# Transposes of q and k in a forgetting attention: from TensorE to VectorE blocks and DMAs through DRAM

## The chip, the core and the metric

The kernel runs on one core of one Trainium2 chip. The metric is the device time of one execution in microseconds (us). The engines of the core that matter here are TensorE (PE in the profile, with PEld for its weight loads), VectorE (DVE), ScalarE (ACT) and SyncE (SP), which issues nearly all DMAs of this kernel from one queue, in order. An engine works through its own instructions in order too, and waits at an instruction until the semaphores that it names have been raised.

## The reference

One layer works on 512 tokens of width 1024: a gated feed-forward network, a mixer, and a second feed-forward network. The mixer multiplies the normed tokens by one wide weight, takes from the product the inputs of an mLSTM with 4 heads and of a forgetting attention with 16 heads of 64, and merges the two by gates. The part that the change touches is the attention:

```python
def forgetting_attention(q, k, v, f_pre, q_g, k_g):
    q = jnp.moveaxis(rms_norm(q, q_g), 1, 2)
    k = jnp.moveaxis(rms_norm(k, k_g), 1, 2)
    ...
    F = jnp.moveaxis(jnp.cumsum(jax.nn.log_sigmoid(f_pre.astype(f32)), axis=1), 1, 2)
    ...
        logits = jnp.einsum('bhqd,bhkd->bhqk', q_blk, k).astype(f32) * scale + (F_blk[..., :, None] - F[..., None, :])
        logits = jnp.where(k_pos[None, :] <= q_pos[:, None], logits, -jnp.inf)
        p = jax.nn.softmax(logits, axis=-1)
        return jnp.einsum('bhqk,bhkd->bhqd', p.astype(v.dtype), v)
```

All is float32. A product is computed by splitting each factor into a high and a low part of a reduced float32 type, and adding three matmuls: high by high, high by low, low by high.

## The kernel before

**Weights.** `raw` (L89 to L93) has SP load a piece of a weight into one of three buffers. `split` (L95 to L105) has ACT copy it to its high part `wh` (L102) and DVE subtract to get the low part `wl` (L104), in four buffers each. `mm3` (L125 to L129) issues the three matmuls, 512 columns wide as a rule.

**The attention's steps.** The 16 heads form four groups of four, and eight pairs. `fox_qkv(g)` (L1119) computes q and k of a group: for each block `tb` of 128 tokens a tile `tk` of 128 tokens by 512 columns, in which columns 0 to 255 are q of the four heads and 256 to 511 are k. DVE moves the product out of PSUM with the bias added (L1127), ACT squares it (L1129), DVE sums the squares (L1130); after all four blocks DVE computes the inverse root of 32 sums per token in eight short instructions (`rsqrt`, L146 to L154) and multiplies each tile by it, in place (L1147, "the norm" below). The same generator then computes v (`vg`, `fvt`, L1158 to L1164). The bias row `bb` is loaded by SP (L1014).

The scores need q and k with the head's 64 columns on the partitions and the tokens along the free axis. `fox_t(p)` (L1184) does this for a pair of heads: PE transposes the pair's 128 columns of q out of the four `tk` tiles into one PSUM bank, and those of k into a second (8 transposes against the identity, L1202). From the banks ACT and DVE make the operands of the scores with the norm's gains: `fq` and `fk` (ACT, L1207 and L1211) and their low parts in `fq` and `klz` (DVE, L1209). `fox_s(h)` computes the scores of a head (PE, L1230 and L1231; DVE, L1233 and L1237, adds the forgetting term that SP has loaded as `A`, L1219; ACT takes the exponential, L1241). `fox_p(h)` divides the rows `S` by their sum (DVE, L1251), has PE transpose them (L1259), and splits them into `Ph` (ACT, L1257) and `Pl` (DVE, L1258). `fox_o(h)` multiplies by v (PE, L1289) and adds up in `yb` (ACT, L1292; DVE, L1293).

**What sets the order.** In `run` a loop over the heads calls these steps for neighbouring heads in turn, and after each call `advance(fill, n)` runs `n` steps of a generator, `fill`. The generator of group g holds the steps of `fox_qkv(g + 1)` and behind them some steps of `gate`, which computes one of 16 gate tiles (PE, then a tanh on ACT, L1333) and has SP store it to DRAM (`g_d`, L1335). In the last heads the fill is `y_a`, which needs four tiles of the tag of `tk` too (`ht`). So the attention's small steps of a group lie between the large matmuls of the next group and of the gates. A scheduler puts each engine's instructions in their order from this program. Tiles of one tag are used again in turn: `tk` has four buffers, so the tiles of a group can be written only when the tiles of the group before have been read for the last time.

```python
        for tb in range(NT):
            t3 = tok[tb].rearrange("p (h d) -> p h d", h=8)
            nc.vector.tensor_tensor(t3, t3, r[:, tb * 8:(tb + 1) * 8].unsqueeze(2).to_broadcast([P, 8, 64]), op=MUL)
```

The names with numbers in the rows of the program below are the tiles: `tk_5965` is one `tk` tile, the number only tells tiles apart.

Of the kernel before, what the change touches and what calls it, by code (L numbers as in the profile page):

```python
# [11 lines left out]
F32 = mybir.dt.float32  # L12
# [8 lines left out]
P = 128  # L21
T = 512
NT = 4
# [24 lines left out]
class Layer:  # L48
    def __init__(self, tc, es, A, out, dbg=None):
        self.tc, self.nc, self.es, self.A, self.out = tc, tc.nc, es, A, out  # L50
        self.dbg = dbg or {}
        pool = lambda name, **k: es.enter_context(tc.tile_pool(name=name, **k))
        self.cp = pool("const", bufs=1)
        self.up = pool("u", bufs=1)
        self.xp = pool("x", bufs=1)
        self.wp = pool("w", bufs=4)
        self.sp = pool("small", bufs=4)
        self.pg = pool("pg", bufs=4, space=PSUM)
        self.pt = pool("pt", bufs=4, space=PSUM)
        self.dp = pool("scr", bufs=1, space=DRAM)  # L60
        self.lo_after = None
        self.n = self.nx = self.now = 0
        self.due = []
        self.free = self.pin = lambda i: i

    def nm(self, s):
# [7 lines left out]
    def tick(self, n=1):  # L74
        for _ in range(n):
            self.now += 1
            for f in [f for t, f in self.due if t == self.now]:
                f()

    def tmp(self, pool, name):  # L80

        return pool.tile([P, 512], F32, name=self.nm(name), tag="t2", bufs=self.ntmp)
# [1007 lines left out]
    def mlstm_h(self, h, ip):  # L1090
# [23 lines left out]
        for tb in range(NT):  # L1114
            nc.vector.tensor_scalar(hs[tb], hs[tb], r[:, tb:tb + 1], None, op0=MUL)
            nc.sync.dma_start(self.h_d[tb * P:(tb + 1) * P, h * 256:(h + 1) * 256], hs[tb])


    def fox_qkv(self, g, ip):  # L1119

        nc, sp, w = self.nc, self.sp, self.A["w_mix"][0]
        o = g * 256
        bb = self.bias_bcast([(QF + o, 256), (KF + o, 256)], ip)
        tok = [ip.tile([P, 512], F32, name=self.nm("tk"), tag="tok", bufs=4) for _ in range(NT)]
        ss = sp.tile([P, NT, 8], F32, name=self.nm("fs"), tag="fs", bufs=2)
        def done(tb, ps):
            nc.vector.tensor_tensor(tok[tb], ps, bb, op=ADD)  # L1127
            j = self.tmp(ip, "fj")
            nc.scalar.activation(j, tok[tb], AF.Square)  # L1129
            nc.vector.tensor_reduce(ss[:, tb, :], j.rearrange("p (h d) -> p h d", h=8), AX.X, ADD)  # L1130
        def mk(ch):
            def make():
                sh = [P, 2, 512]
                rows = w[ch * 256:(ch + 1) * 256]
                r = self.raw(sh, [(lambda t, i=i: t[:, :, i * 256:(i + 1) * 256],
                                   rows[:, c + o:c + o + 256].rearrange("(k p) n -> p k n", p=P))
                                  for i, c in enumerate((QF, KF))])
                wh, wl = self.split(r, sh)
                return wh, wl, 2 * ch, 2
            return make  # L1140
        yield from self.u_gemm_tokens([mk(c) for c in range(4)], 512, done)
        v = sp.tile([P, NT * 8], F32, name=self.nm("fv"), tag="fv", bufs=2)
        nc.vector.tensor_scalar(v, ss.rearrange("p b h -> p (b h)"), 1.0 / 64, EPS, op0=MUL, op1=ADD)
        r = self.rsqrt(v, NT * 8)
        for tb in range(NT):
            t3 = tok[tb].rearrange("p (h d) -> p h d", h=8)
            nc.vector.tensor_tensor(t3, t3, r[:, tb * 8:(tb + 1) * 8].unsqueeze(2).to_broadcast([P, 8, 64]), op=MUL)  # L1147
        if g == 3:
            self.fx[g] = tok, self.fx[g]
            return  # L1150
        gs = ((0,), (1,), (2, 3))[g]
        n = len(gs) * 256
        bv = self.bias_bcast([(VF + o, n)], ip) if g else None
        vts = [ip.tile([P, NT, 4, P], F32R, name=self.nm("fvt"), tag="vm", bufs=3) for _ in gs]
        def donev(tb, ps):
            f = ip.tile([P, n], F32, name=self.nm("vg"), tag="t2", bufs=3)
            if g:
                nc.vector.tensor_tensor(f, ps[:, :n], bv[:, :n], op=ADD)  # L1158
            else:
                nc.sync.dma_start(f, self.v0_d[tb])  # L1160
            for i, vt in enumerate(vts):
                f4 = f[:, i * 256:(i + 1) * 256].rearrange("p (h d) -> p h d", h=4)
                nc.scalar.activation(vt[:, tb, :, 0:64], f4, AF.Copy)
                nc.vector.tensor_tensor(vt[:, tb, :, 64:P], f4, vt[:, tb, :, 0:64], op=SUB)  # L1164
        def mkv(ch):
            def make():
                k = 8 // (2 * len(gs))
                sh = [P, k, n]
                r = self.raw(sh, [(lambda t: t, w[ch * k * P:(ch + 1) * k * P, VF + o:VF + o + n]
                                   .rearrange("(k p) n -> p k n", p=P))])  # L1170
                wh, wl = self.split(r, sh)
                return wh, wl, k * ch, k
            return make
        self.fx[g] = (tok, vts[0])
        if len(gs) > 1:
            self.fx[3] = vts[1]
        if g:
            yield from self.u_gemm_tokens([mkv(c) for c in range(2 * len(gs))], n, donev)
        else:
            for tb in range(NT):  # L1180
                donev(tb, None)
            yield

    def fox_t(self, p, ap):  # L1184


        nc = self.nc
        g, pr = p // 2, p % 2
        tok, vt = self.fx[g]
        if p < 2:  # L1190

            self.klz[p] = [ap.tile([P, T], F32R, name=f"klz{p}{h}", tag="qk", bufs=16) for h in range(2)]
            for h in range(2):
                nc.gpsimd.memset(self.klz[p][h][64 - h * 64:P - h * 64, :].bitcast(F32), 0.0)
        lohi = (slice(0, 64), slice(64, P))
        new = lambda n: ap.tile([P, T], F32R, name=self.nm(n), tag="qk", bufs=16)
        q, k, kl = [new("fq") for _ in range(2)], [new("fk") for _ in range(2)], self.klz[p % 2]
        for i, R in ((0, R_FQ), (1, R_FK)):
            c = i * 256 + pr * P
            b = self.tbank()  # L1200
            for tb in range(NT):
                nc.tensor.transpose(b[:, tb * P:(tb + 1) * P], tok[tb][:, c:c + P], self.ident)  # L1202
            gc = self.colA[:, R + p:R + p + 1]
            for h in range(2):
                own, oth = lohi[h], lohi[1 - h]
                d = (q, k)[i][h]
                nc.scalar.activation(d[own, :], b[own, :], AF.Copy, scale=gc[own, :])  # L1207
                lo = q[h][oth, :] if i == 0 else kl[h][own, :]
                nc.vector.scalar_tensor_tensor(lo, b[own, :], gc[own, :], d[own, :], op0=MUL, op1=SUB)  # L1209
                if i:  # L1210
                    nc.scalar.activation(k[h][oth, :], b[own, :], AF.Copy, scale=gc[own, :])  # L1211
        self.qkt[p] = (q, k, kl)
# [150 lines left out]
    def run(self):  # L1363
        nc, tc, A = self.nc, self.tc, self.A
        gain = lambda r: self.colA[:, r:r + NK]
        self.x_d = self.dp.tile([T, D], F32, name="x_d")
        self.h_d = self.dp.tile([T, D], F32, name="h_d")
        self.v0_d = [self.dp.tile([P, 256], F32, name=f"v0_d{tb}") for tb in range(NT)]
        self.g_d = [self.dp.tile([P, T], F32, name=f"g_d{i}") for i in range(2 * NK)]

        self.ntmp, self.xn_tiles, self.gb_tag = 4, self.xn_ffn, ("gb", 2)
# [2 lines left out]
        with tc.tile_pool(name="f1t", bufs=1) as tp:  # L1374
# [5 lines left out]
            with tc.tile_pool(name="f1h", bufs=1) as hp:  # L1380
# [6 lines left out]
                n = 0  # L1387
# [128 lines left out]
        with tc.tile_pool(name="att", bufs=1) as ip:  # L1516
# [15 lines left out]
            nc.vector.tensor_scalar(self.hgg, self.colA[:, R_GG:R_GG + 2 * NK], 0.5, None, op0=MUL)  # L1532
            self.klz = [None] * 2
            self.vt, self.W, self.fx, self.qkt, self.S = [None] * 4, {}, {}, {}, {}
            def advance(gen, n):
                for _ in range(n):
                    next(gen, None)
            advance(self.v_mlstm(0, ip, ip), 99)

            gates = iter([(m, i) for i in range(2) for m in range(NK)][2:])  # L1540
# [4 lines left out]
            for h0, n, fill in ((0, 3, with_gates(self.v_mlstm(1, ip, ip), 1)), (2, 4, with_gates(self.fox_qkv(0, ip), 3))):  # L1545
                for f, h in ((self.mlstm_w, h0), (self.mlstm_w, h0 + 1), (self.mlstm_h, h0), (self.mlstm_h, h0 + 1)):
                    f(h, ip)
                    advance(fill, n)
                    if f == self.mlstm_h and h == 2:
                        self.fox_t(0, yp)  # L1550
                advance(fill, 99)
            for n in range(18):
                if n % 4 == 0 and n < 16:
                    advance(fill, 99)
                    g = n // 4
# [21 lines left out]
        with tc.tile_pool(name="br", bufs=1) as bp:  # L1577
# [17 lines left out]
            for m in range(NK):  # L1595
                t = self.branch(m, 1, bp, None)
# [21 lines left out]
        with tc.tile_pool(name="f2t", bufs=1) as tp, tc.tile_pool(name="f2h", bufs=1) as hp:  # L1618
# [9 lines left out]
            n = 0  # L1628
# [39 lines left out]
```

## Time and profile before

| | us |
|---|---|
| median of three runs | 1321.18 (1321.18, 1321.39, 1319.3) |
| the profiled execution | 1319.86 |
| its span on the core | 1318.1 |
| PE busy, of the span | 1303.3 |
| DVE busy | 953.4 |
| ACT busy | 630.3 |

A row of the profile's table of groups or of its timeline reads: start in us, length in us, engine, line of the program, operation, tile written <- tiles read, partitions x elements, type, and the count of instructions in the row. An "SPq" row is the issue of a DMA by SP, not its transfer. A bracket at the end is the time that the engine sat idle just before, and what ended it. A row of the table of windows gives a stretch, the busy time of PE, PEld, DVE, ACT and POOL in it with their instructions, the granted clock of PE, the share of time in which the DMA engines were busy, and what they moved in GB/s.

### The profile page before, as it was taken

How to read it: one execution, taken by the hardware profiler on the slowest of the kernel's cores; microseconds unless marked ns; L12 is line 12 of the kernel's file. 1: busy time of each engine (PE TensorE's matmuls, PEld its weight loads, DVE VectorE, ACT ScalarE, POOL GpSimd, SP SyncE). 2: the span in 40 equal slices, each digit the busy share in tenths (PEclk: the TensorE clock that was granted, in tenths of full speed). 3: DMA queues.
4: the chain of work that ended last, by engine and by line, in shares of the span. 5: the costliest groups of instructions: out<-in, count | busy, mean ns of one | idle time of the engine just before them, and what ended most of it. 6: DMA issues, size and time to landing. Idle time of an engine off the chain costs nothing.

```text
span 1318.1 us, 17796 instructions
## 1 busy us (share of the span) xinstructions
PE 1303.3 (99%) x6345; PEld 1092.2 (83%) x6345; DVE 953.4 (72%) x1735; ACT 630.3 (48%) x1056; POOL 36.9 (3%) x57
## 2 busy tenths in 40 slices
PE   7999999999999999999999999999999999999998
PEld 6788888888899888888888788878898888888887
DVE  6877777578788687887887778777567557635787
ACT  5623232355476555566566666334372223223642
POOL 1000000000010101000000000003000000000000
PEclk9999999999999999999999999999999999999999
DMA  9998978465845434533343536777539767634574
GB/s 287 278 316 291 326 265 278 149 198 166 299 120 145 117 104 130 155 106 113 89 121 76 171 98 194 215 255 234 185 104 325 255 232 278 220 104 133 171 263 149
DMA packets 204488, 254.18 MB, mean 193 GB/s; under 512 B 15008, under 2 KB 146752, under 8 KB 204400
## 3 DMA queue, kind: packets, MB, share of 16 engines
q1 hardware_dynamic: 204016, 252.98, 60.1%
q8 instruction: 50, 0.82, 0.3%
q14 instruction: 38, 0.31, 0.1%
q0 software_dynamic: 320, 0.06, 0.0%
q10 hardware_dynamic: 64, 0.02, 0.0%
HBM read 217.28 MB, written 35.72 MB: 192 GB/s over the span
## 4 chain that ended last, share of the span: by engine, by line
PE 86%; DMA 4%; DVE 4%; ACT 3%; SPq 1%; issue 1%; DVEq 0%; ACTq 0%
PE g L129 22%; PE g L127 22%; PE g L128 22%; PE t L127 4%; PE t L129 4%; PE t L128 4%; DMA raw<-in_w_branch_a_dram 2%; PE g L909 1%; PE t L1289 1%; PE t L1259 1%; DMA raw<-in_w_ada_dram 1%; PE t L1230 1%; DVE wl L104 1%; PE t L1231 1%; DMA raw<-in_w_branch_b_dram 1%
## 5 line engine op out<-in xcount | busy, mean ns | idle before, releaser
L102 ACT ACTIVATE wh<-raw 128x1024 fp32r<-128x1024 f32 (+2 forms) x246 | 249.2, 1017 | 378.0 <-PE g L128 118.5
L104 DVE TENSOR_TENSOR wl<-raw,wh 128x1024 fp32r<-128x1024 f32 (+2 forms) x246 | 287.2, 1170 | 163.9 <-ACT wh L102 141.9
L127 PE MATMUL g<-uh,wh 128*128 128x512 f32 (+1 forms) x880 | 341.0, 387 | 0.0
L128 PE MATMUL g<-ul,wh 128*128 128x512 f32 (+1 forms) x880 | 339.5, 386 | 0.4 <-DVE ul L268 0.4
L129 PE MATMUL g<-uh,wl 128*128 128x512 f32 (+1 forms) x880 | 339.6, 386 | 0.0
L129 PEld LDWEIGHTS g<-uh,wl 128*128 128x128 f32 x880 | 165.3, 188 | 33.6
L128 PEld LDWEIGHTS g<-ul,wh 128*128 128x128 f32 x880 | 165.4, 188 | 33.2 <-DVE ul L268 0.6
L127 PEld LDWEIGHTS g<-uh,wh 128*128 128x128 f32 x880 | 165.3, 188 | 32.6 <-issue 0.6
L304 DVE SCALAR_TENSOR_TENSOR acc<-raw,ccol,acc 128x512 f32<-128x512 f32 (+1 forms) x70 | 66.8, 975 | 45.0 <-DMA raw<-in_w_ada_dram 44.9
L127 PE MATMUL g<-wh,uh 128*128 128x512 f32 (+1 forms) x256 | 97.4, 381 | 0.0
L129 PE MATMUL g<-wh,ul 128*128 128x512 f32 (+1 forms) x256 | 96.7, 378 | 0.0
L128 PE MATMUL g<-wl,uh 128*128 128x512 f32 (+1 forms) x256 | 96.4, 377 | 0.0
L127 PE MATMUL t<-wh,A 128*128 128x512 f32 x176 | 68.6, 390 | 0.0
L128 PE MATMUL t<-wl,A 128*128 128x512 f32 x176 | 68.5, 389 | 0.0
L129 PEld LDWEIGHTS g<-wh,ul 128*128 128x128 f32 x256 | 48.2, 188 | 9.1
L127 PEld LDWEIGHTS g<-wh,uh 128*128 128x128 f32 x256 | 48.2, 188 | 8.7 <-DVE tk L1127 0.5
L128 PEld LDWEIGHTS g<-wl,uh 128*128 128x128 f32 x256 | 48.2, 188 | 8.3
L129 PE MATMUL g<-yh,wl 128*128 128x512 f32 x128 | 50.1, 391 | 0.8 <-DVE wl L104 0.8
L127 PE MATMUL g<-yh,wh 128*128 128x512 f32 x128 | 49.9, 390 | 0.0
L128 PE MATMUL g<-yl,wh 128*128 128x512 f32 x128 | 49.8, 389 | 0.0
L420 ACT ACTIVATE A<-E 128x768 fp32r<-128x768 f32 x22 | 18.6, 846 | 55.5 <-DVE E L419 55.5
L1241 ACT ACTIVATE S<-S,mn 128x128 f32<-128x128 f32 (+1 forms) x64 | 35.5, 556 | 16.1 <-DVE mn L1233 9.9
(360 smaller groups left out, 2240.8 us busy)
## 6 DMA issues: line engine op xcount, KB each, us to landing
raw<-in_ffn_w_in_dram SPq DMA_DIRECT2D x82, 512.0 KB, 4.5
raw<-in_w_ada_dram SPq DMA_DIRECT2D x56, 512.0 KB, 5.6
raw<-in_w_mix_dram SPq DMA_DIRECT2D x46, 512.0 KB, 4.3
sa<-in_ffn_w_out_dram SPq DMA_DIRECT2D x22, 512.0 KB, 6.3
sb<-in_ffn_w_out_dram SPq DMA_DIRECT2D x44, 256.0 KB, 6.6
ws<-sa SPq DMA_DIRECT2D x22, 512.0 KB, 4.1
ws<-sb SPq DMA_DIRECT2D x44, 256.0 KB, 4.8
raw<-ws SPq DMA_DIRECT2D x44, 256.0 KB, 3.6
```

The lines of the kernel that those rows point to most:

```text
L102: nc.scalar.activation(hi, src, AF.Copy)
L104: self.last_lo = nc.vector.tensor_tensor(lo, src, hi, op=SUB)
L127: pin(mm(ps, lh, rh, start=start, stop=False))
L128: pin(mm(ps, lh, rl, start=False, stop=False))
L129: self.last_mm = pin(mm(ps, ll, rh, start=False, stop=stop))
L304: nc.vector.scalar_tensor_tensor(a, r[:, s], c, a, op0=MUL, op1=ADD)
L420: nc.scalar.activation(A1[:, 0:3, :], E[:, 0:3, :], AF.Copy)
L909: pin(nc.tensor.matmul(acc_ps[b], (wl if p == 1 else wh)[:, b % 2, s], self.ul[k] if p == 2 else self.uh[k], start=k == 0 and p == 0, stop ...
L1230: nc.tensor.matmul(ps[:, :w], q[:, s], k[:, :w], start=True, stop=False)
L1231: nc.tensor.matmul(ps[:, :w], q[:, s], kl[:, :w], start=False, stop=True)
L1241: nc.scalar.activation(S[:, ws], S[:, ws], AF.Exp, scale=-1.0, bias=m, accum_out=sm[:, qb:qb + 1])
L1259: tr = lambda b, c, qb, kb: nc.tensor.transpose(b[:, c:c + P], S[:, P_OFF[qb] + kb * P:P_OFF[qb] + (kb + 1) * P], self.ident)
```

## The change

For groups 1 to 3 PE no longer transposes q and k. Group 0 keeps its two pairs of transposes. For each later group the following steps take their place:

1. After each tile's norm DVE runs a transpose on the tile in place. It works on square blocks of 32 by 32 elements, each on its own: block (a, b) stays where it is and is transposed inside.
2. One step of the fill later SP stores the four tiles to a DRAM buffer of 512 by 512.
3. Three steps of the fill later SP loads from it four tiles `fT` (q and k of the group's two pairs), which take the four `tk` buffers over. Each tile is loaded by four DMAs of 32 partitions; each partition reads 16 pieces of 32 elements (128 bytes), which puts the blocks in the transposed order.
4. `fox_t` reads the `fT` tiles from SBUF where it read the two PSUM banks.

The steps that store and load hang on a new list, `posts`, which `advance` counts down. The diff, without lines that only rename:

```diff
+    def post(self, steps, f):
+        self.posts.append([steps, f])
+
+    def advance(self, gen, n):
+        for _ in range(n):
+            next(gen, None)
+            for p in self.posts[:]:
+                p[0] -= 1
+                if p[0] < 0:
+                    self.posts.remove(p)
+                    p[1]()
...
+    def blocks(self, t, src):
+
+        for j in range(4):
+            self.nc.sync.dma_start(t[32 * j:32 * j + 32, :].rearrange("a (t b) -> a t b", b=32),
+                                   src[:, 32 * j:32 * j + 32].rearrange("(t a) b -> a t b", a=32))
...
             nc.vector.tensor_tensor(t3, t3, r[:, tb * 8:(tb + 1) * 8].unsqueeze(2).to_broadcast([P, 8, 64]), op=MUL)
+            if g:
+                t = tok[tb]
+                nc.vector.transpose(t, t)
+                self.post(1, lambda t=t, tb=tb: nc.sync.dma_start(self.t_d[g][tb * P:(tb + 1) * P, :], t))
+        def bring():
+            qk = [ip.tile([P, T], F32, name=self.nm("fT"), tag="tok", bufs=4) for _ in range(4)]
+            for n in (0, 2, 1, 3):
+                self.blocks(qk[n], self.t_d[g][:, n * P:(n + 1) * P])
+            self.fx[g][0] = qk
+        if g:
+            self.post(3, bring)
...
-            c = i * 256 + pr * P
-            b = self.tbank()
-            for tb in range(NT):
-                nc.tensor.transpose(b[:, tb * P:(tb + 1) * P], tok[tb][:, c:c + P], self.ident)
+            if g:
+                b = tok[2 * i + pr]
+            else:
+                b = self.tbank()
+                c = i * 256 + pr * P
+                for tb in range(NT):
+                    nc.tensor.transpose(b[:, tb * P:(tb + 1) * P], tok[tb][:, c:c + P], self.ident)
```

The change also moves instructions. Three places follow, each as the engine's rows before and now. In the changed program L1169 is the new transpose, L1170 the store, L1134 the loads; L1166 is the norm, L1282 the division, L1290 the transposes of the rows `S`, L1320 the product with v, L1366 the store of a gate, L1250 the load of `A`, L1027 of `bb`, L105 of a weight.

The first place is PE at the first pair of group 1, before: the last matmul of head 2's product with v, the transposes of the pair's q and k, and those of head 3's rows.

```order
L1289 MATMUL t_5868<-Pl_5748,fvt_5049 128x256
L1202 MATMUL t_5884<-ident,tk_5316 128x128
L1202 MATMUL t_5884<-ident,tk_5317 128x128
L1202 MATMUL t_5884<-ident,tk_5318 128x128
L1202 MATMUL t_5884<-ident,tk_5319 128x128
L1202 MATMUL t_5893<-ident,tk_5316 128x128
L1202 MATMUL t_5893<-ident,tk_5317 128x128
L1202 MATMUL t_5893<-ident,tk_5318 128x128
L1202 MATMUL t_5893<-ident,tk_5319 128x128
L1259 MATMUL t_5913<-ident,S_5610 128x128 x4
```

The same place in the changed program:

```order
L1320 MATMUL t_5900<-Ph_5779,fvt_5053 128x256
L1320 MATMUL t_5900<-Pl_5780,fvt_5053 128x256
L1290 MATMUL t_5935<-ident,S_5618 128x128 x4
L1290 MATMUL t_5942<-ident,S_5618 128x128 x4
L1290 MATMUL t_5949<-ident,S_5618 128x128 x2
L140 MATMUL g_5992<-wh_5999,uh_3271 128x512
```

The eight transposes of the pair are gone, and PE goes from head 2 to head 3's rows at once.

The second place is DVE around the norm of group 2 (tiles `tk_5965` to `tk_5968`, in the changed program `tk_5987` to `tk_5990`), before:

```order
L104 TENSOR_TENSOR wl_6522<-raw_6519,wh_6521 128x1024
L1147 TENSOR_TENSOR tk_5965<-tk_5965,rq_6250 128x512
L1147 TENSOR_TENSOR tk_5966<-tk_5966,rq_6250 128x512
L1147 TENSOR_TENSOR tk_5967<-tk_5967,rq_6250 128x512
L1147 TENSOR_TENSOR tk_5968<-tk_5968,rq_6250 128x512
L1237 ISA S_6308,mn_6309<-t_6328,A_1195_6304,mn_6309 128x384
```

The same place in the changed program, up to the division of head 5's rows:

```order
L1166 TENSOR_TENSOR tk_5988<-tk_5988,rq_6262 128x512
L1169 STREAM_TRANSPOSE tk_5987<-tk_5987 128x512
L1169 STREAM_TRANSPOSE tk_5988<-tk_5988 128x512
L1166 TENSOR_TENSOR tk_5989<-tk_5989,rq_6262 128x512
L1166 TENSOR_TENSOR tk_5990<-tk_5990,rq_6262 128x512
L1169 STREAM_TRANSPOSE tk_5989<-tk_5989 128x512
L1169 STREAM_TRANSPOSE tk_5990<-tk_5990 128x512
L1268 ISA S_6328,mn_6329<-t_6348,A_1195_6324,mn_6329 128x384
L1324 TENSOR_TENSOR yb_3658<-t_6404,yt_6413 64x512
L1282 TENSOR_SCALAR S_6121<-S_6121,sm_6123 128x128
```

Four transposes stand between the parts of the norm, and head 5's division, which stood ahead of the whole group's evacuation before, now stands behind the norm. The four instructions that read pair 3's q and k (L1209, now L1240) have gone the other way: they stood behind the evacuation of group 2 and now stand ahead of it.

The third place is SP's queue where group 3's weights are loaded, before (`raw_6692` and `raw_6735` are the first two pieces of the weight of q and k, each loaded by two DMAs):

```order
L92 DMA raw_6692<-in_w_mix_dram 128x2x256 x2
L1219 DMA A_1256_6650<-A_d 128x512
L92 DMA raw_6735<-in_w_mix_dram 128x2x256 x2
L92 DMA raw_6794<-in_w_mix_dram 128x2x256 x2
L92 DMA raw_6855<-in_w_mix_dram 128x2x256 x2
L1219 DMA A_1291_6813<-A_d 128x512
L1014 DMA bb_6680<-in_b_mix_dram 128x256 x2
L92 DMA raw_6985<-in_w_mix_dram 128x8x128
L1335 DMA g_d_92<-tg_6561 128x512
L92 DMA raw_7049<-in_w_mix_dram 128x8x128
L1335 DMA g_d_93<-tg_6647 128x512
```

The changed program, from the last of the four stores of group 2 on; the first piece of the weight stands ahead of these stores:

```order
L1170 DMA t_d_86<-tk_5990 128x512
L1250 DMA A_1258_6680<-A_d 128x512
L1134 DMA fT_6384<-t_d_86 32x16x32 x4
L1134 DMA fT_6386<-t_d_86 32x16x32 x4
L1134 DMA fT_6385<-t_d_86 32x16x32 x4
L1134 DMA fT_6387<-t_d_86 32x16x32 x4
L1366 DMA g_d_96<-tg_6601 128x512
L1366 DMA g_d_97<-tg_6677 128x512
L1027 DMA bb_6710<-in_b_mix_dram 128x256 x2
L105 DMA raw_6765<-in_w_mix_dram 128x2x256 x2
```

The second piece of the weight (`raw_6735` before, `raw_6765` now) stood ahead of the bias and the gates' stores, and now stands behind the stores of group 2, the 16 loads, two gates' stores and the bias.

More of the change, by code (lines that the diff above doesn't have):

```diff
@@ L63, in __init__ @@
         self.due = []
+        self.posts = []
         self.free = self.pin = lambda i: i
@@ L1147, in fox_qkv @@
             nc.vector.tensor_tensor(t3, t3, r[:, tb * 8:(tb + 1) * 8].unsqueeze(2).to_broadcast([P, 8, 64]), op=MUL)
+            if g:
[9 more added lines that the diff above has]
+            self.post(3, bring)
         if g == 3:
-            self.fx[g] = tok, self.fx[g]
             return
@@ L1173, in mkv @@
             return make
-        self.fx[g] = (tok, vts[0])
-        if len(gs) > 1:
-            self.fx[3] = vts[1]
+        for i, vt in zip(gs, vts):
+            self.fx[i] = [tok, vt]
         if g:
@@ L1368, in run @@
         self.v0_d = [self.dp.tile([P, 256], F32, name=f"v0_d{tb}") for tb in range(NT)]
+        self.t_d = [self.dp.tile([T, 512], F32, name=f"t_d{g}") for g in range(4)]
         self.g_d = [self.dp.tile([P, T], F32, name=f"g_d{i}") for i in range(2 * NK)]
@@ L1534, in run @@
             self.vt, self.W, self.fx, self.qkt, self.S = [None] * 4, {}, {}, {}, {}
-            def advance(gen, n):
-                for _ in range(n):
-                    next(gen, None)
+            advance = self.advance
             advance(self.v_mlstm(0, ip, ip), 99)
```

## The prediction

> **What bounds the kernel now.** I read the page's table of engines first, then its chain of waits by engine.
>
> ```profile
> PE 1303.3 (99%) x6345; PEld 1092.2 (83%) x6345; DVE 953.4 (72%) x1735; ACT 630.3 (48%) x1056; POOL 36.9 (3%) x57
> PE 86%; DMA 4%; DVE 4%; ACT 3%; SPq 1%; issue 1%; DVEq 0%; ACTq 0%
> ```
>
> TensorE is busy for 99% of the span and carries 86% of the chain. A share over the whole span says little of one stage, so next the table of windows over the stretch with groups 1 to 3 (PE, PEld, DVE, ACT, POOL, granted clock, DMA share, GB/s):
>
> ```profile
> 580.00:630.00 50.00, 49.90 (x280) 42.98 (x279) 41.38 (x118) 29.87 (x69) 0.00 (x0) 1.00 0.38 114
> 630.00:680.00 50.00, 49.85 (x254) 41.13 (x253) 42.99 (x109) 32.50 (x66) 0.00 (x0) 1.00 0.35 101
> 680.00:730.00 50.00, 49.98 (x249) 41.46 (x248) 36.53 (x94) 29.58 (x62) 0.00 (x0) 1.00 0.36 96
> ```
>
> PE has no hole there and its granted clock is full, so a microsecond taken from PE is a microsecond of the kernel, as long as nothing that PE waits for comes later. But DVE is busy for 73% to 86%, and it gets new work. The DMA engines are idle for more than half of the time.
>
> **What is removed.** 48 of the 64 transposes. The view of their line and the timeline of PE at pair 4:
>
> ```profile
> L1202 PE MATMUL t<-ident,tk x64: 270/272/273, 534.1 to 744.4; 128*128 128x128 f32 x64
> 670.05 0.39 PE L129 MATMUL g<-uh,wl 128*128 128x512 f32 x1
> 670.28 1.03 PE L1202 MATMUL t<-ident,tk 128*128 128x128 f32 x8
> 671.16 1.04 PE L1259 MATMUL t<-ident,S 128*128 128x128 f32 x8
> ```
>
> The first row invites 48 x 0.272 = 13.1 us. That is wrong: records on PE overlap. The 512-wide matmul lasts 0.39 us, yet the next instruction starts 0.23 after it. What a burst of eight transposes takes from PE is start to start: 671.16 - 670.28 = 0.88. Six bursts go: **-5.3 us**. That is all that can be gained.
>
> **What VectorE gets.** 12 transposes of 128x512. None is in this trace. The rows of DVE at the norms of groups 1 and 2, and what stands around the second:
>
> ```profile
> 586.38 2.48 DVE L1147 TENSOR_TENSOR tk<-tk,rq 128x512 f32<-128x512 f32 x4
> 627.06 1.27 DVE L1251 TENSOR_SCALAR S<-S,sm 128x128 f32<-128x128 f32 x4
> 628.43 1.23 DVE L104 TENSOR_TENSOR wl<-raw,wh 128x1024 fp32r<-128x1024 f32 x1
> 634.64 1.89 DVE L1127 TENSOR_TENSOR tk<-g,bb 128x512 f32<-128x512 f32 x3 [4.38 <-PE t L1202]
> 650.15 2.50 DVE L1147 TENSOR_TENSOR tk<-tk,rq 128x512 f32<-128x512 f32 x4
> 652.56 0.62 DVE L1237 CUSTOM_DVE_ANT_0 S<-t,A,mn 128x384 f32<-128x384 f32 x1
> 652.90 0.93 PE L1259 MATMUL t<-ident,S 128*128 128x128 f32 x7
> L1209 DVE SCALAR_TENSOR_TENSOR klz<-t,colA,fk 64x512 fp32r<-64x512 f32 x16 | 12.0, 750 | 2.3 <-ACT fk L1207 1.8
> ```
>
> An instruction over 128x512 floats in SBUF takes 0.62 (2.48 / 4); one over twice as many columns takes 1.23. I take 0.6, since the shape is the same, and keep 1.23 as the upper bound; nothing excludes a little less. So 2.4 us per group, 7.2 in all, up to 14.8. [...]
>
> Where does it reach PE? At group 2. Today the first three evacuations into `tk` wait 4.38 us for PE's transposes of pair 3, which hold the buffers; behind them DVE runs nearly without a gap to 652.56, when the norm is done. Head 5's division stands ahead of it all (627.06), long before PE's transposes of its rows at 652.90. Now it stands behind the norm. Both streams come 1.76 earlier (two bursts): PE wants the rows at 651.1. For DVE: 652.56 - 1.76 = 650.8; four instructions of 0.75 on pair 3 (L1209) move ahead into the idle 4.38 (-3.0); two of the three evacuations (0.63 each) start as soon as their banks are full (-1.3); then four transposes (+2.4), the row of 0.62, a `yb` of about the same, and the division (1.27): 651.4. That is 0.3 late, with the hand-overs I take **+0.8**. If neither the early evacuation comes nor the transposes stay at 0.6 but take 1.23: 0.8 + 1.3 + 2.5 = 4.6. The lower bound is 0. At group 1 the later DVE work is on the path of the next part; group 3's stretch has DVE at 73%, which hides 2.4 of 50.
>
> **Group 1: the way through DRAM.** Pair 2 is wanted soonest after its norm. The rows: PE's transposes, ACT's first read, the first score; issues with us to landing; the shortest comparable issue; and two short windows with small packets.
>
> ```profile
> 602.98 1.03 PE L1202 MATMUL t<-ident,tk 128*128 128x128 f32 x8
> 603.95 0.68 ACT L1207 ACTIVATE fq<-t,colA 64x512 fp32r<-64x512 f32 x1
> 609.15 0.39 PE L1230 MATMUL t<-fk,fq 128*128 128x256 f32 x1
> g_d<-tg SPq DMA_DIRECT2D x14, 256.0 KB, 2.0
> x_d<-x SPq DMA_DIRECT2D x16, 256.0 KB, 2.7
> L808 SPq DMA_DIRECT2D ar<-in_w_ada_dram x32: 378/562/1141, 4.9 to 41.2; - x32
> 377.20:378.50 1.30, 1.30 (x14) 1.30 (x13) 1.30 (x4) 1.30 (x4) 0.87 (x1) 1.00 0.71 82
> DMA packets 1277, 0.11 MB, mean 82 GB/s; under 512 B 1216, under 2 KB 1276, under 8 KB 1276
> 553.60:556.60 3.00, 3.00 (x15) 2.49 (x14) 1.74 (x6) 1.06 (x1) 0.00 (x0) 1.00 0.91 268
> DMA packets 1166, 0.80 MB, mean 268 GB/s; under 512 B 36, under 2 KB 1019, under 8 KB 1166
> ```
>
> Wanted: from `fq` (603.95) to the score (609.15) are 5.2 us; the score comes 0.9 earlier without the burst, so `fq` must start by 603.0. Ready: the norm ends at 586.38 + 2.48 = 588.9, with four transposes at 591.2; a store of 256 KB lands 2.0 to 2.7 after its issue, so at about 593.8. Then eight loads bring the pair's two tiles, at 0.4 to 0.56 us of issue each (L808), with 32 packets of 128 bytes each on every one of 16 engines, and the last lands 2.0 later: 593.8 + 256 p + 2.0, p the price of a packet. Below: 1277 packets, nearly all under 512 bytes, went in 1.3 us, 16 x 1.3 / 1277 = 16.3 ns each. Above: 0.80 MB in 3 us at share 0.91 is 16 x 3 x 0.91 / (0.80 MB / 512 B), 28 ns per 512 bytes. So 600.0 to 603.0, against 603.0: **+0.3** for collisions with weights. Past 28 ns every further nanosecond costs 0.256 us here.
>
> **Group 2: SP's queue.** The second piece of group 3's weight now stands behind the 16 loads, two gates' stores and the bias.
>
> ```profile
> 650.31 11.21 SPq L92 DMA_DIRECT2D raw<-in_w_mix_dram  x6
> 665.83 0.82 SPq L1014 DMA_DIRECT2D bb<-in_b_mix_dram  x2
> 677.88 0.39 PE L129 MATMUL g<-uh,wl 128*128 128x512 f32 x1
> 679.88 0.69 ACT L1333 ACTIVATE tg<-g,hgg 128x512 f32<-128x512 f32 x1
> 680.60 0.33 SPq L1335 DMA_DIRECT2D g_d<-tg  x1
> raw<-in_w_mix_dram SPq DMA_DIRECT2D x33, 256.0 KB, 3.1
> 685.12 1.06 ACT L102 ACTIVATE wh<-raw 128x1024 fp32r<-128x1024 f32 x1 [2.17 <-PE g L129]
> 686.68 0.60 ACT L1292 ACTIVATE yt<-t 64x512 f32<-64x512 f32 x1
> 686.21 0.40 PE L127 MATMUL g<-wh,uh 128*128 128x512 f32 x1
> ```
>
> It was issued near 650 and used from 686.21. Now SP waits for the tanh of the second gate, whose last matmul starts at 677.88. From there: matmul 0.39, tanh 0.69, store 0.33, bias 0.82, issue 0.44, landing 3.1, high part 1.06, low part 1.23, an allowance of 0.6 for hand-overs: 8.7 us, or 10.3 if the tanh again starts 1.6 after its matmul (679.88). PE has 686.21 - 677.88 = 8.3 us of work until the weight, and 2.2 more that the new order puts ahead of it (ten transposes of rows at 0.11, two narrow scores, four matmuls of the first piece at 0.23): 10.5. It fits, barely. But on ACT the high part now stands behind `yt`, which waits for head 6's product: 0.60 + 1.06 + 1.23 + 0.3 of hand-overs = 3.2 against 2.2 of PE work: **+0.9**, bounds 0 and 2.5 (tanh late as well).
>
> **Group 3.** Norm at 722.61, PE's transposes of both pairs at 742.79: 20 us, against 2.4 + 0.3 + 2.7 + 2.0 and 512 packets of 16 to 28 ns (8.3 to 14.3). Nothing.
>
> ```profile
> 722.61 2.49 DVE L1147 TENSOR_TENSOR tk<-tk,rq 128x512 f32<-128x512 f32 x4
> 742.79 1.91 PE L1202 MATMUL t<-ident,tk 128*128 128x128 f32 x16
> ```
>
> Sum: -5.3 + 0.3 + 0.8 + 0.9 = **-3.3**. The profiled execution took 1319.86, so 1316.6 for such a one; the median of the runs is 1.3 above it: 1321.18 - 3.3 = **1317.9**. By the bounds (0 and 0.3 against 4.6 + 2.5 + 0.3) the sum lies between -5.3 and +2.1.
>
> **The rivals.**
>
> B, given back: the new order costs PE about what it gains. Between the norm and the last load SP issues 20 DMAs per group, 16 of which can begin only when the stores have landed, and each load of a weight behind them is late. With the DVE term at 2.1 (no early evacuation), the queue's at 2.5 and one weight late by 0.7 elsewhere the costs are 5.3 and the sum is 0: **1321**. For it: PE's cover at the weight is 10.5 against 8.7 to 10.3. Against it: weights have three buffers and are mostly issued well ahead.
>
> C, slower through the pieces: a packet of 128 bytes costs more than one of 512. It decides from 28 ns, and turns the sign at about 41 (3.3 / 0.256 = 13 above). At 60 ns: group 1 32 x 0.256 = +8.2; group 2 (norm done near 648, loads done at about 655 + 15.4 against 668.5 wanted) +2; group 3 (720.7 + 2.4 + 5.0 + 15.4 = 743.5 for pair 6, wanted about 742.5) +1; with the other terms -5.3 + 8.2 + 2 + 1 + 0.8 + 0.9 + 1 of late weights = +8.6: **1330**. Against it: the small packets above at 16 ns. [...]
>
> D, VectorE becomes the bound: 1.23 per transpose. Group 2 +4.6 instead of 0.8, group 3 +2.5, group 1 unchanged (600.0 + 2.5 = 602.5 at 16 ns, wanted 603.0), queue +0.9: -5.3 + 0.3 + 4.6 + 2.5 + 0.9 = +3.0: **1324**. It costs from about 1.0 us per transpose on. Against it: the norm's 0.62.
>
> **How the numbers follow.** Forecast 0.46, own range 1315.5 to 1319.5; B 0.26; C 0.17; D 0.11. A measurement of this kernel tells about 0.2% (2.6 us) from no change, so the forecast counts as faster, B as the same, C and D as slower: 0.46, 0.26, 0.28. The range takes in the whole gain of 5.3 with the runs' spread below, B, D and the half of C under 45 ns (+5 to +7) above: 1314.5 to 1328.
>
> **What would show it.** Line L1169 at 0.6 us and 12 instructions; the stores and loads of group 1 done before 603; PE starting the first score of pair 2 without idle; division L1282 of head 5 followed at once by PE's transposes; the second weight of group 3 less than 1 us late on PE; PE's busy time down by the 48 transposes and the span down by less. The prediction is wrong if `fq` of pair 2 waits for `fT` for microseconds, if a transpose lasts over 1 us, or if weights behind the loads make PE wait.

## The result and the profile after

The changed kernel took 1317.52 us (median of 11 runs), the kernel before 1320.19 (median of 11). Over all runs but one of the kernel before, a slow one of 2657.2 us, the ratio is 0.9975, with a 95% interval of 0.9967 to 0.9984. That is 3.3 us less, between 2.1 and 4.4; the two medians themselves differ by 2.7. The forecast was a sum of -3.3 us, or 1317.9.

The profiled execution took 1316.01, with a span of 1314.2, 3.9 less than before. The page's table of engines and its chain of waits, after:

```profile
PE 1296.7 (99%) x6297; PEld 1087.8 (83%) x6297; DVE 960.1 (73%) x1747; ACT 631.6 (48%) x1056; POOL 36.9 (3%) x57
PE 83%; DVE 6%; DMA 5%; ACT 3%; issue 2%; SPq 1%; DVEq 0%; ACTq 0%
```

The 48 transposes are gone from PE (6345 to 6297 matmuls), and 12 instructions and 6.7 us have come to DVE. The chain, 86% PE before, has given up 3% to DVE, DMA and the rest: PE now waits in places where it did not. The windows say where (the last row is of the kernel before, for the stretch that the prediction did not show):

```profile
580.00:630.00 50.00, 49.80 (x279) 43.39 (x279) 42.94 (x123) 33.97 (x76) 0.00 (x0) 1.00 0.50 130
630.00:680.00 50.00, 50.00 (x250) 42.30 (x249) 46.68 (x124) 33.00 (x72) 0.00 (x0) 1.00 0.46 119
680.00:730.00 50.00, 49.35 (x244) 41.33 (x244) 42.56 (x100) 28.61 (x57) 0.00 (x0) 1.00 0.65 177
730.00:780.00 50.00, 47.79 (x247) 40.46 (x246) 35.16 (x102) 35.01 (x74) 0.00 (x0) 1.00 0.55 157
```

```profile
730.00:780.00 50.00, 49.28 (x260) 40.89 (x259) 36.94 (x100) 34.49 (x74) 0.00 (x0) 1.00 0.49 146
```

PE loses 0.65 us in the stretch behind group 2 and 2.2 in the one behind group 3, where it lost 0.7 before. Over the four stretches PE is idle for 3.1 us, before for 1.0. In PE's timeline two waits stand out:

```profile
684.54 0.39 PE L1261 MATMUL t<-fk,fq 128*128 128x256 f32 x1 [0.59 <-DVE yb L1324]
773.86 0.50 PE L1261 MATMUL t<-fk,fq 128*128 128x512 f32 x1 [2.21 <-DVE mn L1264]
```

The first, behind the head's product with v, is a wait for a PSUM bank that the product still holds until `yb` has read it. The second, 2.2 us by the records and 2.4 by the starts, over the usual step, comes after the matmul of 771.32, in the middle of a head's scores, and again is a wait for a bank: DVE has not read the scores yet. The rows of ACT, DVE and SP at that place (and two rows of SP from 20 us earlier) show why:

```profile
749.92 0.33 SPq L1366 DMA_DIRECT2D g_d<-tg  x1
751.27 0.50 SPq L105 DMA_DIRECT2D raw<-in_w_mix_dram  x1
767.29 0.38 SPq L105 DMA_DIRECT2D raw<-in_w_mix_dram  x1
771.28 1.06 ACT L115 ACTIVATE wh<-raw 128x1024 fp32r<-128x1024 f32 x1 [2.92 <-DMA raw<-in_w_mix_dram]
772.37 1.23 DVE L117 TENSOR_TENSOR wl<-raw,wh 128x1024 fp32r<-128x1024 f32 x1 [2.01 <-ACT wh L115]
773.51 0.28 DVE L1264 CUSTOM_DVE_ANT_0 S<-t,Am 128x128 f32<-128x128 f32 x1
```

A weight is late; ACT waits 2.92 us for it; DVE waits at that weight's low part, and the scores' evacuation (L1264), which has nothing to do with the weight, stands behind it. PE has the scores of three blocks in the banks and stops at the fourth. The weight is late because SP issued it at 767.29. Up to 749.92 SP had stood at gates' stores for most of 20 us, each time until a tanh was done (18.6 us in three waits from 725 on). Just ahead of 767.29 it waited 1.8 us for something else: until DVE had read an earlier weight (L117) and so freed one of the three `raw` buffers. That this late buffer goes back to the gates' stores is an inference here; an experiment below moves these stores.

The parts of the way through DRAM came as forecast or better. The new transpose, the first store and the first load of group 1, and ACT's first read of a loaded tile:

```profile
L1169 DVE STREAM_TRANSPOSE tk<-tk x12: 665/688/710, 588.1 to 715.9; 128x512 f32<-128x512 f32 x12
588.88 3.31 SPq L1170 DMA_DIRECT2D t_d<-tk  x4
594.48 8.50 SPq L1134 DMA_DIRECT2D fT<-t_d  x16
599.63 0.71 ACT L1238 ACTIVATE fq<-fT,colA 64x512 fp32r<-64x512 f32 x1
```

And the view of the DMA queues in the 9.5 us from 594.5 to 604, with the loads of group 1:

```profile
DMA packets 8520, 1.30 MB, mean 137 GB/s; under 512 B 8272, under 2 KB 8517, under 8 KB 8517
q1 hardware_dynamic: 8517, 1.28, 80.6%
```

A packet of a load took 16 x 9.5 x 0.806 / 8517 = 14.4 ns, and the first tile was read at 599.63, where 603.0 would have been in time.

### The profile page after: what moved, and what is told of

The parts are those of the page before. It is cut to its first block, busy times and chain, and to the rows that moved or that the text cites. A ratio compares the mean times of both kernels' runs of the same rounds, so it can differ in the third digit from the quotient of the medians.

```text
span 1314.2 us, 17824 instructions
## 1 busy us (share of the span) xinstructions
PE 1296.7 (99%) x6297; PEld 1087.8 (83%) x6297; DVE 960.1 (73%) x1747; ACT 631.6 (48%) x1056; POOL 36.9 (3%) x57
## 4 chain that ended last, share of the span: by engine, by line
PE 83%; DVE 6%; DMA 5%; ACT 3%; issue 2%; SPq 1%; DVEq 0%; ACTq 0%
PE g L142 21%; PE g L141 21%; PE g L140 21%; PE t L140 4%; PE t L141 4%; PE t L142 4%; DMA raw<-in_w_branch_a_dram 2%; PE g L922 1%; DMA raw<-in_w_mix_dram 1%; DVE wl L117 1%; ACT wh L115 1%; PE t L1320 1%; DVE acc L317 1%; PE t L1290 1%; PE t L1261 1%
## 5 line engine op out<-in xcount | busy, mean ns | idle before, releaser
L117 DVE TENSOR_TENSOR wl<-raw,wh 128x1024 fp32r<-128x1024 f32 (+2 forms) x246 | 288.0, 1173 | 164.2 <-ACT wh L115 142.3
L433 ACT ACTIVATE A<-E 128x768 fp32r<-128x768 f32 x22 | 18.6, 845 | 50.9 <-DVE E L432 50.9
```

The source lines that it names most:

```text
L117: self.last_lo = nc.vector.tensor_tensor(lo, src, hi, op=SUB)
L433: nc.scalar.activation(A1[:, 0:3, :], E[:, 0:3, :], AF.Copy)
```

## The experiments

All are the changed kernel with one edit, except the control, which is the kernel before with one, and the last, which has two. Ratios are to the kernel before, run beside them.

**The gain alone.** No vector transposes, no stores, no loads; `fox_t` reads the `tk` tiles.

```diff
-                nc.vector.transpose(t, t)
-                self.post(1, lambda t=t, tb=tb: nc.sync.dma_start(self.t_d[g][tb * P:(tb + 1) * P, :], t))
...
-        if g:
-            self.post(3, bring)
         if g == 3:
+            self.fx[g][0] = tok
             return
```

> The changed kernel without the vector transposes, the stores and the loads: fox_t of groups 1 to 3 reads the tk tiles as they are, so q and k of these groups are not transposed at all. What is left is the change's gain alone. Theory (PE's time is the kernel's time, a burst of eight transposes is worth 0.88 us): 5.3 us under before, between 4.5 and 6.5 with the small stalls that stood beside the bursts, so about 1315 against 1320.2. Rival one (the records' 0.272 us a transpose are PE time): 13 us under before, 1307. Rival two (the bursts filled time in which PE would have waited anyway): less than 3 us under before.

Measured: 1313.63 us, ratio 0.9949 (0.9936 to 0.9963): 6.7 us less, between 4.9 and 8.4; by the medians beside it (1319.62) 6.0. Burst and not record is the price of a transpose on PE. The interval holds the forecast's 5.3 too. If the gain is larger, the rest has a likely place in the trace of before: behind the transposes of pairs 6 and 7, PE waited for the operands that ACT and DVE were still making from the banks:

```profile
747.50 0.63 PE L1259 MATMUL t<-ident,S 128*128 128x128 f32 x4 [0.28 <-DVE fq L1209]
752.12 0.44 PE L1259 MATMUL t<-ident,S 128*128 128x128 f32 x2 [0.30 <-ACT fk L1211]
```

PE's row before the first starts at 746.83 and the one before the second at 751.43, so that over their usual 0.23 they cost 0.44 and 0.46 us; with a third of 0.31 at 754.72 that is 1.2. In this run the stretch from 730 to 780 has PE busy for all of its 50.00 us. But the run also has a wait that neither kernel has, 0.99 us for `yb` ahead of the scores at 607.11, so it is not quite the gain and nothing else.

So the changed kernel gives back about 3.4 us (0.26%) of what it gains; with both intervals, anything from about 1 to 5.5. The next two ask to which part.

**One part of the new way at a time.** The vector transposes without the DMAs (the edit above without its first line), and the DMAs without the vector transposes (its first line alone).

> The changed kernel with the 12 vector transposes but without the stores and loads through DRAM; fox_t reads the tk tiles, transposed within blocks only, so q and k of groups 1 to 3 stay in a wrong order. Theory (the vector transposes lie beside PE's work and cost up to 0.8 us): within 1 us of the kernel with nothing instead. Rival (VectorE is what gives back the change's 1.6 to 2 us of new stalls): within 1 us of the changed kernel, 1317.5, and 2 us or more over the kernel with nothing instead.

> The changed kernel without the 12 vector transposes: the tiles go through DRAM untransposed within their blocks, so q and k of groups 1 to 3 come in a wrong order. Theory (the new stalls come from the DMAs: from SP's queue and from the tiles that come later): about the time of the changed kernel, 1316.5 to 1317.5, with stalls of PE over 0.5 us still in the stretch from 680 to 780 us. Rival (they come from VectorE): about the time of the kernel with nothing instead, 1315.

Measured: 1313.09, ratio 0.9949 (0.9937 to 0.9962), and 1312.52, ratio 0.9949 (0.9935 to 0.9962). Neither costs anything that can be measured over the gain alone, though the intervals leave room for some 2 us. The first was expected, the second was not: with the DMAs by themselves PE is busy for all 100 us from 680 to 780, without either wait. It takes both. A comparison of SP's queue behind group 2 shows how, first of the changed kernel, then of the one with the DMAs alone:

```profile
645.40 3.30 SPq L1170 DMA_DIRECT2D t_d<-tk  x4
650.62 9.25 SPq L1134 DMA_DIRECT2D fT<-t_d  x16
669.03 6.86 SPq L1366 DMA_DIRECT2D g_d<-tg  x2
675.99 0.88 SPq L1027 DMA_DIRECT2D bb<-in_b_mix_dram  x2
676.91 1.96 SPq L105 DMA_DIRECT2D raw<-in_w_mix_dram  x4
```

```profile
642.38 2.13 SPq L1169 DMA_DIRECT2D t_d<-tk  x4
646.65 8.53 SPq L1134 DMA_DIRECT2D fT<-t_d  x16
669.02 0.34 SPq L1365 DMA_DIRECT2D g_d<-tg  x1
669.46 0.87 SPq L1027 DMA_DIRECT2D bb<-in_b_mix_dram  x2
670.38 0.94 SPq L105 DMA_DIRECT2D raw<-in_w_mix_dram  x2
```

Without the vector transposes the tiles are stored 3 us earlier, and the scheduler puts the bias and the second piece of the weight ahead of the second gate's store; SP issues them at 670. With both parts it puts them behind, SP is held at the gates' stores for 6.86 us, and the weight is issued at 676.91.

Behind group 3 it is ACT's order that differs. The last matmul of the last of these gates starts at 745.23 in the changed kernel and at 744.10 with the DMAs alone; the rows of its tanh are these, the changed kernel's first:

```profile
749.20 0.69 ACT L1364 ACTIVATE tg<-g,hgg 128x512 f32<-128x512 f32 x1
```

```profile
744.53 0.69 ACT L1363 ACTIVATE tg<-g,hgg 128x512 f32<-128x512 f32 x1 [0.45 <-PE g L142]
```

With the DMAs alone ACT waits for the gate. In the changed kernel the tanh stands behind two exponentials of the scores and two reads of `fT`, which run from 746.22 on. SP issues the next weight behind its store at 751.27 instead of 746.09.

**The gates' stores off SP's queue,** in the changed kernel and, as a control, in the kernel before:

```diff
-            nc.sync.dma_start(self.g_d[8 * i + m], th)
+            nc.scalar.dma_start(self.g_d[8 * i + m], th)
```

> The changed kernel with the gates' stores issued by ScalarE's queue, where the tanh runs, so that SP's weights, biases and h tiles never wait for a tanh. Theory (the stalls of 1.1 us near 684 and 2.4 us near 771 are weights that stood behind gates' stores on SP): both are gone, 2 to 4 us under the changed kernel, 1313.5 to 1315.5. Rival one (they are the order of the small steps, on VectorE and in PSUM banks): within 1 us of the changed kernel, 1317.5, with stalls of the same size. Rival two (issuing costs ScalarE more than SP's wait costs): slower than the changed kernel.

> The kernel before with the gates' stores issued by ScalarE's queue: the control for the run with the changed kernel. Theory (before the change SP's weights stand ahead of the gates' stores, so that nothing waits): within 1 us of before, 1319.6. Rival (SP's waits cost both kernels alike): 2 us or more under before.

Measured: 1313.14, ratio 0.9936 (0.9923 to 0.9949), 8.4 us less than before (6.7 to 10.2); and for the control 1321.12, ratio 1.0004 (0.9996 to 1.0012). The interval of the first lies wholly under that of the changed kernel: this version beats both, and it gains more than 5.3. The stretch behind group 3, of the moved stores in the changed kernel:

```profile
730.00:780.00 50.00, 50.00 (x265) 42.67 (x264) 35.76 (x98) 35.16 (x74) 0.00 (x0) 1.00 0.56 163
```

PE does not wait. The late steps' weights that the changed kernel's SP issued at 751.27 and 767.29 (the latter is the one that ACT waited for) are issued here, 8 to 9 us sooner, in a program that is some 2 us ahead:

```profile
741.87 0.37 SPq L105 DMA_DIRECT2D raw<-in_w_mix_dram  x1
759.10 0.38 SPq L105 DMA_DIRECT2D raw<-in_w_mix_dram  x1
```

So the loss is SP's order: in the kernel before SP stands at these stores for 34.0 us in all from 640 to 775, and that holds up nothing that is needed; in the changed one it does. Two things are left open. The edit also lets the scheduler shift small steps of other engines, so that a share of the 5 us may be theirs. And SP is not wholly free of the gates: the trace still puts two of its waits ahead of a weight between 655 and 735, 12.7 us together, down to a gate's store that has not landed; PE is busy throughout from 630 to 780.

**Group 3 back on PE,** groups 1 and 2 changed:

```diff
-            if g:
+            if 0 < g < 3:
                 t = tok[tb]
...
-        if g:
+        if 0 < g < 3:
             self.post(3, bring)
...
-            if g:
+            if 0 < g < 3:
                 b = tok[2 * i + pr]
```

> The changed kernel with group 3 transposed by TensorE again: 32 of 64 transposes gone instead of 48, no loads of group 3 on SP. Theory (group 3's way through DRAM holds up the weights of the steps after it): 1.8 us of PE time come back and the 2.4 us near 771 go, so within 1 us of the changed kernel, 1317.5. Rival (that stall has nothing to do with group 3): 1.5 us or more over the changed kernel, 1319.

Measured: 1316.32, ratio 0.9965 (0.9953 to 0.9976), 1.2 us under the changed kernel's median, just past the theory's 1 us and far from the rival's 1319. The wait at 771 is gone; the one at 684 stands, with the same length and the same releaser:

```profile
684.73 0.38 PE L1262 MATMUL t<-fk,fq 128*128 128x256 f32 x1 [0.59 <-DVE yb L1325]
```

The two waits belong to the two groups behind which they lie. Group 3 loses about what it earns; whether a little more, the intervals do not tell.

**More of the vector transpose:** two and three in place of each one.

```diff
                 nc.vector.transpose(t, t)
+                nc.vector.transpose(t, t)
```

> The changed kernel with each vector transpose done twice (which undoes it, so q and k of groups 1 to 3 come in a wrong order): 12 more of 0.69 us, so that a transpose costs 1.38, a little more than the price of rival D. The kernel with three took about 17 us more than the changed one, with stalls at groups 2 and 3 of 6 to 9 us each. Theory (VectorE has about 3 us to spare per group after the change, 50 - 46.7 in the fullest window, and the second transpose takes 2.75): 1 to 4 us over the changed kernel, 1318.5 to 1321.5. Rival one (no spare time, every microsecond of VectorE is one of the kernel): 8 us over, 1325. Rival two (the threefold kernel lost its time elsewhere): no difference.

> The changed kernel with each of the 12 vector transposes done three times in place (three make one), so 24 more of 0.69 us, 5.5 us more of VectorE per group. Theory (VectorE has 3 to 7 us to spare in 50 at each group, and what is late there reaches PE through the rows' division and the scores): 2 to 6 us slower than the changed kernel, 1319.5 to 1323.5. Rival one (VectorE's time is fully hidden): within 1 us of the changed kernel. Rival two (VectorE is already the bound): 12 us or more slower than the changed kernel.

Measured: with two 1323.41, ratio 1.0017 (1.0008 to 1.0025); with three 1336.29, ratio 1.0119 (1.0104 to 1.0133). Against the changed kernel that is 5.9 and 18.8 us by the medians, for 8.3 and 16.5 us of VectorE. The theory had said 1 to 4 and 2 to 6; with three the second rival's 12 or more came. But this is not VectorE's time alone. Where PE paused, its granted clock fell. In the profiled execution with two it was 0.84 in the 6 us from 676 and 0.69 in the 8 us behind them (last section), which is 3.4 us of PE's work; with three it was 0.93 in each of the two stretches from 630 to 730, which is 7.0:

```profile
630.00:680.00 50.00, 44.98 (x206) 36.20 (x204) 48.44 (x127) 30.51 (x69) 0.00 (x0) 0.93 0.33 80
680.00:730.00 50.00, 45.80 (x207) 37.57 (x208) 35.43 (x84) 25.31 (x47) 0.00 (x0) 0.93 0.61 160
```

That leaves some 2.5 and 12 us by estimate, the first within what the theory had said, the second above it. The longest wait of PE with two, and what held it:

```profile
667.63 8.57 SPq L1367 DMA_DIRECT2D g_d<-tg  x2
676.25 0.42 SPq L1251 DMA_DIRECT2D A<-A_d  x1
680.87 0.69 DVE L1254 TENSOR_TENSOR Am<-A,maskF 128x512 f32<-128x512 f32 x1 [2.16 <-DMA A<-A_d]
682.15 0.77 PE L1321 MATMUL t<-Ph,fvt 128*128 128x512 f32 x1 [5.76 <-DVE mn L1265]
```

Again SP at the gates' stores, this time with a forgetting term behind them. That led to the last experiment, both edits together:

> Both edits at once: each vector transpose done twice (which undoes it, so q and k of groups 1 to 3 come in a wrong order) and the gates' stores on ScalarE's queue. In the run with the doubled transposes alone the longest stall of TensorE, 5.9 us at 676, ended with a forgetting term A that SP had issued only behind two gates' stores. Theory (VectorE's time reaches TensorE through SP's queue, not by itself): most of the 5.5 us that the doubling cost the changed kernel is gone, within 2.5 us of the kernel with the gates' stores moved, 1313 to 1316. Rival (VectorE itself is short of time): 4 us or more over that kernel, 1317 or more.

Measured: 1321.38, ratio 1.0012 (1.0003 to 1.0021), 8 us by the medians over the kernel with the gates' stores moved. The theory falls, the rival's 4 us or more came. The longest wait of PE is now DVE's own:

```profile
648.05 1.26 DVE L1170 STREAM_TRANSPOSE tk<-tk 128x512 f32<-128x512 f32 x2
650.35 1.20 DVE L117 TENSOR_TENSOR wl<-raw,wh 128x1024 fp32r<-128x1024 f32 x1
651.61 0.50 PE L141 MATMUL g<-wl,uh 128*128 128x512 f32 x1 [2.96 <-DVE wl L117]
```

DVE works through norm and eight transposes from 642.05 to 649.24 without a pause, and a weight's low part behind them lets PE wait for 2.96 us. The next longest, 1.89 us ahead of 680.87, is not DVE's: DVE had waited 1.05 us for `fk`, which ACT made behind a gate's tanh and its store. The lower clock behind that pause took another 1.7 (last section). SP is not out of it either: its weights of 675.83 had waited up to 6.4 us, by the trace until a gate's store had landed. One transpose per tile fits beside PE's work, two do not; how much of the 8 us is DVE's time alone stays open.

## Why the prediction was right

**The bound.** PE's time was the kernel's. Taking the bursts away, with nothing in their place, gave 6.0 us by the medians and 6.7 by the ratio, and the records' 13.1 was wrong, as argued.

**The term of 5.3** was too small, by about 1. The run with nothing in place of the bursts does not show this clear of noise; the run with the gates' stores moved does, with 6.7 us or more, if moving them gains nothing by itself, as in the control. Bursts are only PE's part of a transpose. The likely rest is the way from the bank through ACT and DVE to the next PE instruction, which cost 1.2 us at pairs 6 and 7 and went too, since the tiles lie in SBUF long before.

**VectorE, +0.8 at group 2.** Not there. A transpose took 0.69 by its records and 0.61 start to start (588.15 to 589.37 for two), as the norm's row had said, and PE did not wait for head 5's division.

**Group 1, +0.3.** PE waited once, for `fk`: the first score of pair 2 starts at 608.18, 0.59 after the matmul ahead of it instead of 0.23. In the profile of before a wait of 0.34, found in the same way, stands at 604.21. So nothing, net. The sum had said 600.0 to 603.0 for both tiles of the pair. The q tile was read at 599.63; the last load of the k tile was issued at 598.24, and ACT first read that tile at 606.66, without having been idle just before. When it landed is not shown.

**SP's queue behind group 2, +0.9.** Right in place; that the size was met is luck in part. Of ACT's order it was right in detail; the rows of the changed kernel:

```profile
683.18 0.60 ACT L1323 ACTIVATE yt<-t 64x512 f32<-64x512 f32 x1
683.68 1.04 ACT L115 ACTIVATE wh<-raw 128x1024 fp32r<-128x1024 f32 x1
684.75 1.23 DVE L117 TENSOR_TENSOR wl<-raw,wh 128x1024 fp32r<-128x1024 f32 x1 [0.26 <-ACT wh L115]
686.03 0.50 PE L141 MATMUL g<-wl,uh 128*128 128x512 f32 x1
```

The high part stands behind `yt`, and PE waits for the low part, but for 0.2 us only. The larger share, 0.59 of idle time, is the wait for `yb` just ahead of it, which the forecast had not seen: ten transposes of rows and a score stand there in a row, with no matmuls of a weight between them to cover the bank. Together they are the 0.8.

**Group 3, nothing.** This is the step that failed. The forecast compared the tiles' arrival with their use, 20 us against a sum of 15.7 to 21.7 by its own terms (7.4 and the packets' 8.3 to 14.3), with the norm's 2.5 not counted. So at its upper price "nothing" did not follow for the last tiles. With packets at 14.4 ns the tiles were in time: PE has no wait from 690 to 771. It did not follow SP's queue beyond them, as it had done for group 2, to the gates' stores, the `h` tiles and the weights of the last heads. That cost 2.4 us at 771. It is one of the signs that the forecast had named for being wrong: weights behind the loads made PE wait. The errors cancel: the gain was 1.4 larger than forecast, group 1 and VectorE cost 1.1 less, group 3 cost 2.4 more. In place of -5.3 + 0.3 + 0.8 + 0.9 the runs and the trace have -6.7 + 0 + 0 + 0.8 + 2.4 = -3.5, beside the measured -3.3. With the medians' 6.0 in place of 6.7 the sum is -2.8, beside their -2.7. So the sum was met by luck, not by each term. Two slips in the forecast's sums change nothing of this: by its own list the lower bound is -5.0 and not -5.3, and B's costs of 5.3 leave out the 0.3 of group 1.

**The rivals.** B was the right mechanism at about two thirds of its price (5.3): a queue in order, in which weights stand behind stores that wait, gave back 3.4 us of 6.7. C fell by its own row: a packet of 128 bytes took 14.4 ns, less than the lower bound of 16.3. The bytes did come more slowly, 128 in 14.4 ns where the forecast's rows gave 512 in 28, but no run shows a packet at the 60 ns of C's sum. D did not happen. Where its condition was made true, with 1.38 us per tile, the kernel took 0.17% more than before, 2.2 us (1.1 to 3.3), and D had said +3.0 at 1.23. That is near, but by another way: a forgetting term was late and not the division, and the clock's 3.4 is in it, which D did not have.

## What to carry to other kernels

A transpose taken from PE, busy for 99% of the span, was worth here about its start-to-start time (0.11 us), and probably the wait for what is made from its result, not its record (0.27). The costs are in the queues that the replacement passes: follow an in-order DMA queue to the end of the stage, and look for a store that waits for a late result with loads behind it; give such stores the queue of the engine that makes the result (here 0.33 us of ACT's queue each). DVE, busy for 73% of the whole span but for 46.7 of the 50 us from 630 to 680, hid little more here: of 8.3 us more on it 5.9 came back, the clock's share included.

## What was not expected of the hardware

In these runs a pause of PE could cost more than its length, and the longer of two pauses was not always the dearer. In the run with doubled transposes the granted clock was lower at and behind the pause of 5.8 us:

```profile
670.00:676.00 6.00, 6.00 (x35) 5.18 (x33) 4.99 (x12) 3.67 (x7) 0.00 (x0) 1.00 0.01 1
676.00:682.00 6.00, 0.39 (x2) 0.00 (x0) 2.48 (x6) 2.90 (x5) 0.00 (x0) 0.84 0.81 187
682.00:690.00 8.00, 7.65 (x24) 5.87 (x25) 7.17 (x22) 6.21 (x12) 0.00 (x0) 0.69 0.74 228
690.00:700.00 10.00, 10.00 (x53) 8.43 (x52) 6.19 (x9) 4.69 (x9) 0.00 (x0) 1.00 0.85 231
```

That is 0.16 of 6 us and 0.31 of 8, or 3.4 us of PE's work. The matmuls show it as well: the first two of these start 0.43 us ahead of the next one, the third 0.23:

```profile
686.05 0.63 PE L141 MATMUL g<-wl,uh 128*128 128x512 f32 x1
686.48 0.59 PE L142 MATMUL g<-wh,ul 128*128 128x512 f32 x1
686.91 0.40 PE L140 MATMUL g<-wh,uh 128*128 128x512 f32 x1
687.14 0.40 PE L141 MATMUL g<-wl,uh 128*128 128x512 f32 x1
```

In the run with both edits a short pause was followed by a lower clock and a longer one was not. The pause of 2.96 us before 651.61, quoted above, was followed by full clock; this one of 1.89 us by half of it, in the stretch from 682 to 684:

```profile
680.87 0.66 PE L1321 MATMUL t<-Ph,fvt 128*128 128x512 f32 x1 [1.89 <-DVE mn L1265]
```

```profile
648.00:652.00 4.00, 1.03 (x5) 0.54 (x4) 4.00 (x9) 1.42 (x4) 0.00 (x0) 1.00 0.35 131
652.00:660.00 8.00, 8.00 (x42) 6.71 (x41) 6.90 (x16) 3.54 (x6) 0.00 (x0) 1.00 0.94 155
680.00:682.00 2.00, 1.13 (x3) 0.97 (x4) 1.97 (x13) 1.70 (x7) 0.00 (x0) 0.75 1.00 310
682.00:684.00 2.00, 2.00 (x10) 2.00 (x10) 1.03 (x5) 2.00 (x5) 0.00 (x0) 0.50 0.78 293
684.00:686.00 2.00, 2.00 (x13) 1.82 (x12) 1.99 (x5) 1.98 (x5) 0.00 (x0) 0.90 0.09 7
686.00:688.00 2.00, 2.00 (x10) 1.62 (x10) 2.00 (x3) 1.98 (x5) 0.00 (x0) 1.00 0.89 284
```

The shorter pause cost 0.25, 0.50 and 0.10 of 2 us each, or 1.7 us of PE's work, beside its own length. In the changed kernel itself the pause of 2.21 us cost no clock:

```profile
771.00:774.00 3.00, 0.79 (x6) 0.47 (x5) 1.63 (x6) 2.37 (x4) 0.00 (x0) 1.00 0.30 87
774.00:780.00 6.00, 6.00 (x29) 5.08 (x30) 4.17 (x19) 3.46 (x11) 0.00 (x0) 1.00 0.31 87
```

What decides whether the clock falls behind a pause is not shown; its length alone does not, since 1.89 us did it and 2.21 and 2.96 did not. The profiled execution of the run for the gain alone had a mean clock of 0.999 and took 1315.65 us, its four others 1.0 and 1312.36 to 1313.71, so the spans of single executions do not compare these kernels.
